# A hybrid encoder layer on one core: the scans' keys stored by step, and the broadcast rows of gates, maxima and factors fetched with one transfer per direction

## The chip, the cores and the metric

The kernel runs on one core of one Trainium2 chip. The core has a matrix engine (PE, whose weight loads are PEld), a vector engine (DVE), an activation engine (ACT), a general engine (POOL) and a queue engine (SP) that issues the transfers. Sixteen DMA engines carry the transfers. The metric is the device time of one execution in microseconds (us), lower is better.

## The reference, cut to what matters

One layer: a combined input projection feeds three head groups, whose outputs are concatenated, projected and added; then cross attention and a squared-ReLU MLP follow. What the change touches are the two scans, each run forward and backward over 16 double chunks of 128 tokens.

```python
h = rmsnorm(x, norm_mix_w[l])
... = jnp.split(h @ w_in[l], IN_OFFSETS, axis=-1)
y_na = neighbourhood_attention(...)      # local attention, 6 heads of 64
y_ml = mlstm_mixer(...)                  # 4 heads of 64, chunks of 64, two directions
y_gd = gated_deltanet_mixer(...)         # 6 heads of 64, chunks of 64, two directions
x = x + jnp.concatenate([y_na, y_ml, y_gd], axis=-1) @ w_out[l]
x = x + memory_cross_attention(...)
x = x + jnp.square(jax.nn.relu(h @ w_ff1[l])) @ w_ff2[l]

# inside gdn_direction, chunk by chunk
wk = jnp.einsum('bhnls,bhnsd->bhnld', t, kb * jnp.exp(gc)[..., None])
q_dec = q * jnp.exp(gc)[..., None]
# inside mlstm_direction, chunk by chunk
s_intra = jnp.einsum('bhnld,bhnsd->bhnls', q, k) * jnp.exp(dmat - m_t[..., None])
a_inter = jnp.exp(inter - m_t)
```

Here `gc` are the running sums of the gates, `m_t` the running maxima, `a_inter` the factors of the carried state.

## The kernel before

The program has two big parts. `mix` computes the three head groups; `tail` does the output projection, the cross attention and the MLP, and is nearly all matmul. `mix` again has two passes. `pass_a` projects the input, forms the chunks' matrices (`gram`, `inv`, `ml_prep`) and writes what the scans need to DRAM. `pass_b` runs the scans and the local attention, and reads it back.

`pass_b` is a loop over 16 steps that calls four generators by turns: `gdn_scan` (one step: chunk pair m forward and chunk pair 15 - m backward), `ml_scan` (the same for the other scan, one step later), `na` (three pieces of the local attention per step, 48 in all), and from step 9 on `heads_out`. The local attention so stands between scan steps and fills the engines. A scheduler with a model of the times turns the program into one order for each engine; each engine then runs its own list in order and waits on semaphores. All transfers of this part are issued by SP, in one list.

Each scan loads its step in a function `load(m)`, one step ahead. Both directions share a tile: one direction has partitions 0 to 63, the other 64 to 127 (`CH`, and `SR` for the other halves). Four of the tiles are filled by one transfer each for both directions:

- `kb` (scaled keys, 128 partitions x 768 floats, L645), from `kb_d`, which is laid out direction first, then step. The two rows wanted, forward m and backward 15 - m, are rows m and 31 - m of 32, so the source is a slice with a stride and has 2 as its outermost size, then 64 x 768.
- `ge` (running sums of gates, L646): one row of 768 floats per direction, repeated over 64 partitions; the source is 2 x 64 (repeated) x 768.
- `me` (running maxima, L850): the same with 512 floats.
- `mge` (factors of the state, L851): the same with 512 floats.

`kb`, `ge`, `qe`, `me`, `mge`, `mqe` and `mkq` have one buffer each, so the load of a step waits until the step before has read them. ACT takes the exponential of `ge` (L647), then POOL multiplies it into the queries (L650). DVE subtracts `me` from the column maxima (L852), POOL adds the mask (L853), ACT takes the exponential (L854), and DVE multiplies (L869). PE reads `kb` in L658. `both` (L664 to L666) is a helper that only issues the transfer, so the page puts `kb` and `ge` at L666.

In the last step, m = 15, the two rows of `kb_d` are rows 15 and 16, which lie side by side; there the `kb` transfer is one of 128 x 768 without the outer 2.

Of the kernel before, what the change touches and what calls it, by code (L numbers as in the profile page):

```python
# [38 lines left out]
class Trunk:  # L39
# [59 lines left out]
    def mix(self):  # L99

        tc, nc, I, dr = self.tc, self.nc, self.I, self.dr
        dt = lambda name, shape: dr.tile(shape, F32, name=name)
        self.y_d = [dt(f"y_d{b}", [8, P, 512]) for b in range(4)]
        self.gd_c = dt("gd_c", [9, P, T])
        self.gate_d = dt("gate_d", [5, P, T])
        self.mlc_d = dt("mlc_d", [16, P, 4, P])
        self.mlv_d = dt("mlv_d", [16, P, 4, 65])
        self.nac_d = dt("nac_d", [6, P, T])
        self.nav_d = dt("nav_d", [T, 384])
        self.g_row = dt("g_row", [16, 2, 2, 6, 64])  # L110
        self.sc_d = dt("sc_d", [2, 16, 2, 64, 2, 6, 64])
        self.kb_d = dt("kb_d", [2, 16, 64, 2, 6, 64])
        self.g_st = dt("g_st", [2, 16, 2, 6, 64])
        self.v_d = dt("v_d", [16, 2, 64, 6, 64])
        self.x_d = dt("x_d", [384, 64, 64])
        self.w_d = [[dt(f"w_d{d}{g}", [64, 12 * (b - a), 64]) for g, (a, b) in enumerate(GROUPS)] for d in range(2)]
        self.wt_d = [dt(f"wt_d{d}", [192, 32, 32]) for d in range(2)]
        with ExitStack() as big:
            self.c = big.enter_context(self.pool("mixc", 1))
            c = self.c  # L120
            self.ind2 = self.load_const("ind2", [P, 2])
            self.gmask = self.load_const("gmask", [P, 2, 64])
            self.egl = c.tile([P, 4, 2, 2, 4, 6], F32, name="egl")
            self.rr = c.tile([P, 16, 12], F32, name="rr")
            self.gcm = c.tile([P, 2, 16, 4], F32, name="gcm")
            self.gtm = c.tile([P, 2, 16, 4], F32, name="gtm")
            self.cm = c.tile([P, 2, 16, 4], F32, name="cm")
            self.cmx = c.tile([P, 2, 16, 4], F32, name="cmx")
            self.wxx = c.tile([P, 2, 16, 4], F32, name="wxx")
            self.emt = c.tile([P, 2, 16, 4], F32, name="emt")  # L130
            self.pass_a()
            self.pass_b()
# [282 lines left out]
    def gram(self, t):  # L415

        nc, pool = self.nc, self.tp
# [3 lines left out]
        e = pool.tile([P, 2, 6, 64], F32, name="gr")  # L421
# [49 lines left out]
        for d in range(2):  # L471
            sc = pool.tile([P, 3, 6, 64], F32, name="sc")
            V.tensor_tensor(out=byp(sc[:, 0]), in0=gv[:, :, :, 0:64], in1=byp(e[:, d]), op=ALU.mult)
            V.tensor_tensor(out=sc[:, 1], in0=heads(kt), in1=col(kst[:, d]), op=ALU.mult)
            V.tensor_tensor(out=sc[:, 2], in0=heads(kt), in1=col(self.eg[:, t, d]), op=ALU.mult)
            nc.sync.dma_start(out=self.sc_d[d, t].rearrange("c s a h l -> (c s) (a h l)"), in_=sc[:, 0:2].rearrange("p a h l -> p (a h l)"))
            for c2 in range(2):
                nc.sync.dma_start(out=self.kb_d[d, t, :, c2], in_=sc[64 * c2:64 * c2 + 64, 2])

    def inv(self, g, dirs, late=False):  # L480

# [140 lines left out]
    def gdn_scan(self, pool):  # L622
# [4 lines left out]
        nc, dr = self.nc, self.dr  # L627
        V, G = nc.vector, nc.gpsimd
        CH = (slice(0, 64), slice(64, 128))
        SR = (slice(64, 128), slice(0, 64))  # L630

        def load(m):
            wp = pool.tile([P, 2, 2, 6, 64], F32, name="wp")
            sc = pool.tile([P, 2, 2, 3, 6, 64], F32, name="sc")
            kb = pool.tile([P, 2, 6, 64], F32, name="kb", bufs=1)
            ge = pool.tile([P, 2, 6, 64], F32, name="ge", bufs=1)
            qe = pool.tile([P, 6, P], F32, name="qe", bufs=1)
            for d in range(2):
                t = m if d == 0 else 15 - m
                g = next(g for g, (a, b) in enumerate(GROUPS) if a <= t < b)  # L640
                nc.sync.dma_start(out=wp[CH[d], d].rearrange("p c h l -> p (c h) l"), in_=self.w_d[d][g][:, 12 * (t - GROUPS[g][0]):12 * (t - GROUPS[g][0]) + 12])
                nc.sync.dma_start(out=sc[CH[d], d, :, 0:2].rearrange("p c a h l -> p c (a h l)"), in_=self.sc_d[d, t].rearrange("c s a h l -> s c (a h l)"))
                nc.sync.dma_start(out=sc[CH[d], d, :, 2].rearrange("p c h l -> p c (h l)"), in_=self.v_d[t].rearrange("c s h l -> s c (h l)"))
                nc.sync.dma_start(out=qe[SR[d]], in_=self.gd_c[0:3, :, P * t:P * t + P].rearrange("c (h e) l -> e (c h) l", h=2))
            both(kb.rearrange("p c h l -> p (c h l)"), self.kb_d.rearrange("d t s c h l -> (d t) s (c h l)")[m:32 - m:31 - 2 * m])  # L645
            both(ge.rearrange("p c h l -> p (c h l)"), self.g_st.rearrange("d t c h l -> (d t) (c h l)")[15 - m:17 + m:2 * m + 1, None].broadcast_to([2, 64, 768]))  # L646
            nc.scalar.activation(out=ge, in_=ge, func=AF.Exp)  # L647
            for d in range(2):
                t = m if d == 0 else 15 - m
                G.tensor_tensor(out=sc[SR[d], d, :, 0], in0=qe[SR[d]].rearrange("p h (c l) -> p c h l", c=2), in1=ge[SR[d]], op=ALU.mult)  # L650
                V.tensor_tensor(out=sc[SR[d], d, :, 1], in0=self.ident[SR[d], None, None, SR[d]].broadcast_to([64, 2, 6, 64]),
                                in1=self.egl[SR[d], t // 4, :, d, t % 4, :, None].broadcast_to([64, 2, 6, 64]), op=ALU.mult)
            for i in range(2):
                ps = self.sps.tile([P, 512], F32, name="pss")
                for h in range(6):
                    for d in range(2):
                        c2 = i if d == 0 else 1 - i
                        nc.tensor.matmul(out=ps[SR[d], 64 * h:64 * h + 64], lhsT=kb[CH[d], c2, h], rhs=wp[CH[d], d, c2, h], start=True, stop=True)  # L658
                for d in range(2):
                    c2 = i if d == 0 else 1 - i  # L660
                    nc.scalar.copy(out=wp[SR[d], d, c2], in_=ps[SR[d], :384].rearrange("p (h x) -> p h x", x=64))
            return wp, sc

        def both(out, in_):  # L664

            nc.sync.dma_start(out=out, in_=in_)  # L666

        cur = load(0)
        yield
        for d in range(2):  # L670
            V.memset(cur[1][SR[d], d, d, 2], 0.0)
        evac = (V.tensor_copy, nc.scalar.copy)
        for m in range(16):
            nxt = load(m + 1) if m < 15 else None
            wp, sc = cur
            for i in range(2):
# [147 lines left out]
    def ml_scan(self, pool):  # L824
        tc, nc, dr = self.tc, self.nc, self.dr
        V, G = nc.vector, nc.gpsimd
        CH = (slice(0, 64), slice(64, 128))
        SR = (slice(64, 128), slice(0, 64))
# [7 lines left out]
        def load(m):  # L836

            sc = pool.tile([P, 2, 2, 2, 4, 64], F32, name="msc")
            r = pool.tile([P, 2, 2, 4, 65], F32, name="mr_")
            qe = pool.tile([P, 4, P], F32, name="mqe", bufs=1)  # L840
            ge = pool.tile([P, 4, P], F32, name="mge", bufs=1)
            kq = pool.tile([P, 2, 4, P], F32, name="mkq", bufs=1)
            e = pool.tile([P, 2, 4, 64], F32, name="me", bufs=1)
            for d in range(2):
                t = m if d == 0 else 15 - m
                nc.sync.dma_start(out=kq[:, d], in_=self.mlc_d[t])  # L846
                nc.sync.dma_start(out=r[CH[d], d].rearrange("p c h x -> p c (h x)"), in_=self.mlv_d[t].rearrange("(c s) h x -> s c (h x)", c=2))
                for a in range(2):
                    nc.sync.dma_start(out=qe[SR[d], a::2], in_=self.mlc_d[t, CH[a], 0:2])
            nc.sync.dma_start(out=e.rearrange("p c h l -> p (c h l)"), in_=self.mx_row.rearrange("d t c h l -> (d t) (c h l)")[m:32 - m:31 - 2 * m, None].broadcast_to([2, 64, 512]))  # L850
            nc.sync.dma_start(out=ge.rearrange("p h l -> p (h l)"), in_=self.ai_row.rearrange("d t h c l -> (d t) (h c l)")[15 - m:17 + m:2 * m + 1, None].broadcast_to([2, 64, 512]))  # L851
            V.tensor_tensor(out=e, in0=self.cmx[:, :, m, :, None].broadcast_to([P, 2, 4, 64]), in1=e, op=ALU.subtract)  # L852
            G.tensor_tensor(out=e, in0=e, in1=gm[:, None, None, :].broadcast_to([P, 2, 4, 64]), op=ALU.add)  # L853
            nc.scalar.activation(out=e, in_=e, func=AF.Exp)  # L854
# [16 lines left out]
            for d in range(2):  # L871
                t = m if d == 0 else 15 - m
# [3 lines left out]
            return sc, r  # L876

        cur = load(0)
        for d in range(2):
            V.memset(cur[1][SR[d], d, d], 0.0)  # L880
        evac = (V.tensor_copy, nc.scalar.copy)
        for m in range(16):
            nxt = load(m + 1) if m < 15 else None
            sc, r = cur
            for i in range(2):
# [531 lines left out]
```

## Time and profile before

| what | value |
|---|---|
| time before, median of 2 runs | 4129.35 us (4127.84 to 4130.86) |
| the profiled execution's own time | 4129.29 us |
| its span, first to last instruction | 4127.3 us |
| mean granted TensorE clock | 0.897 |
| busy: PE, PEld, DVE, ACT, POOL | 85%, 69%, 43%, 27%, 35% |
| transfers of queue 1 (SP's) | 375816 packets, 421.79 MB |

The page shows each engine's busy time over 40 slices, the transfers, the chain of work that ended last, and the costliest groups. In a group's row "x16" is the count; "a <- b" in a list of waits means that a stood idle until b was done. The chain names, step by step from the end back, what the work had waited for; a transfer in it counts from its issue to its landing. "SPq" is SP issuing a transfer.

### The profile page before, as it was taken

Reading aid. Unit: us, or ns where it says so; the run is one execution under the profiler, and the core shown is the slowest. Engines: PE = TensorE matmul, PEld = TensorE weight load, DVE = VectorE, ACT = ScalarE, POOL = GpSimd, SP = SyncE. Lnnn points to the kernel's source line nnn. Section 1 sums busy time; section 2 is a strip of 40 time slices with the busy share of each in tenths; the row PEclk is TensorE's granted clock in tenths of the full one; section 3 lists DMA queues with packets and bytes.
Section 4 is the critical chain, followed back from the end, with each engine's and each line's share of the span. In section 5 each row is a group of like instructions: output and inputs, shape, how many; then the busy total and the mean of one; then the engine's idle time right before and its main releaser. Section 6 shows DMA issues by size and latency. Waiting matters only on the chain.

```text
span 4127.3 us, 53735 instructions
## 1 busy us (share of the span) xinstructions
PE 3515.8 (85%) x21360; PEld 2830.8 (69%) x21360; DVE 1770.1 (43%) x3241; ACT 1122.2 (27%) x1976; POOL 1435.5 (35%) x876
## 2 busy tenths in 40 slices
PE   5988999895357566663999999999999999999998
PEld 4766777673235454442888888778888877888887
DVE  7767483741243345555443434532222244222224
ACT  3222422231122222221343333322221232221123
POOL 4242523441121112223544544433333354333333
PEclk8989999995576766775999999999999999999999
DMA  4476425855343454533333333321111132111112
GB/s 134 114 197 135 152 83 160 228 117 140 94 113 91 114 144 118 137 110 129 112 97 127 98 120 131 106 78 46 45 49 51 55 104 83 44 46 47 51 51 87
DMA packets 376610, 426.79 MB, mean 103 GB/s; under 512 B 150872, under 2 KB 277544, under 8 KB 374696
## 3 DMA queue, kind: packets, MB, share of 16 engines
q1 hardware_dynamic: 375816, 421.79, 34.8%
q8 instruction: 168, 2.75, 0.3%
q0 software_dynamic: 544, 1.57, 0.2%
q14 instruction: 82, 0.67, 0.1%
HBM read 331.16 MB, written 92.12 MB: 103 GB/s over the span
## 4 chain that ended last, share of the span: by engine, by line
PE 56%; DMA 13%; DVE 4%; SPq 3%; issue 2%; POOL 2%; ACT 1%; DVEq 0%; POOLq 0%; ACTq 0%
PE psg L95 31%; PE psa L95 19%; DMA ge<-g_st 4%; DMA me<-mx_row 3%; DMA wp<-w_d 1%; DMA y_d<-gz 1%; PE psn L977 1%; SPq L953 1%; PE psy L997 1%; PE psn L987 1%; DMA sc<-sc_d 1%; SPq L846 1%; DMA nav<-nav_d 0%; PE pss L688 0%; POOL wlo L1021 0%
## 5 line engine op out<-in xcount | busy, mean ns | idle before, releaser
L1021 POOL TENSOR_TENSOR wlo<-wraw,whi 128x1024 fp32r<-128x1024 f32 (+2 forms) x386 | 773.1, 2004 | 1367.0 <-ACT whi L1019 1328.7
L95 PE MATMUL psg<-acta,whi 128*128 128x512 f32 (+1 forms) x3008 | 951.9, 397 | 6.4 <-ACT acta L1160 3.2
L95 PE MATMUL psg<-actb,whi 128*128 128x512 f32 (+1 forms) x2752 | 841.6, 388 | 49.0 <-ACT actb L273 14.0
L1019 ACT CAST whi<-wraw 128x1024 fp32r<-128x1024 f32 (+2 forms) x402 | 358.1, 891 | 1230.6 <-PE psa L95 556.8
L95 PEld LDWEIGHTS psg<-acta,whi 128*128 128x128 f32 (+1 forms) x3008 | 567.8, 190 | 129.6 <-ACT acta L1160 4.0
L95 PE MATMUL psa<-ht,whi 128*128 128x512 f32 x2048 | 638.7, 395 | 0.7 <-ACT whi L1019 0.7
L95 PEld LDWEIGHTS psg<-actb,whi 128*128 128x128 f32 x2752 | 515.1, 192 | 158.1 <-ACT actb L273 14.7
L95 PE MATMUL psg<-acta,wlo 128*128 128x512 f32 (+1 forms) x1504 | 595.8, 397 | 1.8 <-POOL wlo L1021 1.8
L95 PE MATMUL psg<-actb,wlo 128*128 128x512 f32 (+1 forms) x1376 | 533.0, 387 | 4.7 <-POOL wlo L1021 4.2
L95 PEld LDWEIGHTS psa<-ht,whi 128*128 128x128 f32 x2048 | 384.1, 188 | 95.1 <-ACT whi L1019 1.6
L95 PE MATMUL psa<-ht,wlo 128*128 128x512 f32 x1024 | 400.8, 396 | 0.5 <-POOL wlo L1021 0.5
L1252 DVE TENSOR_TENSOR fr<-fr 128x512 f32<-128x512 f32 x128 | 167.8, 1311 | 495.6 <-ACT fr L1251 495.6
L1265 DVE TENSOR_TENSOR xb<-psa,xb 128x512 f32<-128x512 f32 x256 | 175.6, 691 | 475.9 <-PE psa L95 475.9
L95 PEld LDWEIGHTS psg<-acta,wlo 128*128 128x128 f32 (+1 forms) x1504 | 286.1, 190 | 64.4 <-POOL wlo L1021 3.3
L95 PEld LDWEIGHTS psg<-actb,wlo 128*128 128x128 f32 x1376 | 263.2, 191 | 57.4 <-POOL wlo L1021 5.8
L1255 POOL TENSOR_TENSOR ht<-fr,ht 128x512 fp32r<-128x512 f32 x128 | 168.9, 1320 | 250.2 <-ACT ht L1254 248.9
L95 PEld LDWEIGHTS psa<-ht,wlo 128*128 128x128 f32 x1024 | 192.2, 188 | 47.4 <-POOL wlo L1021 1.7
L853 POOL TENSOR_TENSOR me<-me,gm 128x512 f32<-128x512 f32 x16 | 21.1, 1320 | 456.9 <-DVE me L852 414.4
L987 PE MATMUL psn<-ident,nas 128*96 128x128 f32 (+1 forms) x336 | 75.6, 360 | 111.6 <-ACT nas L983 111.4
L308 DVE SCALAR_TENSOR_TENSOR acc<-pad,vecs,acc 128x512 f32<-128x512 f32 (+2 forms) x144 | 143.8, 1012 | 2.8
L1048 DVE TENSOR_TENSOR ss<-ss,sqt 128x512 f32<-128x512 f32 (+1 forms) x91 | 120.4, 1324 | 45.1 <-ACT sqt L1047 42.2
L997 PE MATMUL psy<-nap,nav 96*64 96x128 f32 (+2 forms) x672 | 89.3, 349 | 52.1 <-ACT nap L990 47.8
(376 smaller groups left out, 4042.3 us busy)
## 6 DMA issues: line engine op xcount, KB each, us to landing
wraw<-in_w_ff SPq DMA_DIRECT2D x72, 512.0 KB
wraw<-in_w_ff SPq DMA_DIRECT2D x144, 256.0 KB
wraw<-in_w_out SPq DMA_DIRECT2D x32, 512.0 KB
wraw<-in_w_xq SPq DMA_DIRECT2D x32, 512.0 KB
wraw<-in_w_xo SPq DMA_DIRECT2D x32, 512.0 KB
wraw<-in_w_gd SPq DMA_DIRECT2D x24, 512.0 KB
sc_d<-sc SPq DMA_DIRECT2D x32, 384.0 KB
sc<-sc_d SPq DMA_DIRECT2D x32, 384.0 KB
```

Source lines behind the costliest of these rows:

```text
L95: nc.tensor.matmul(out=out, lhsT=a(k), rhs=b(k), start=(i == 0), stop=(i == n - 1))
L308: V.scalar_tensor_tensor(out=acc[:, :n], in0=pad[:, p0 + j:p0 + j + n], scalar=cw(j), in1=acc[:, :n], op0=ALU.mult, op1=ALU.add)
L846: nc.sync.dma_start(out=kq[:, d], in_=self.mlc_d[t])
L953: nc.sync.dma_start(out=vw[:rows * ncl, j], in_=src)
L987: nc.tensor.transpose(out=tp[:n, P * j:P * j + P], in_=s[:, kt * j:kt * j + n], identity=self.ident)
L997: nc.tensor.matmul(out=yp[64 * e:64 * e + 64, P * hp:P * hp + P], lhsT=vw[:n, j, 128 * hp + 64 * e:128 * hp + 64 * e + 64], rhs=pts[e][:n, ...
L1019: nc.scalar.copy(out=hi, in_=raw)
L1021: (lo_eng or nc.gpsimd).tensor_tensor(out=lo, in0=raw, in1=hi.bitcast(F32), op=ALU.subtract)
L1048: nc.vector.tensor_tensor(out=ss, in0=ss, in1=sq, op=ALU.add)
L1252: V.tensor_tensor(out=r, in0=r, in1=r, op=ALU.mult)
L1255: G.tensor_tensor(out=ht[:, 1], in0=r, in1=ht[:, 0].bitcast(F32), op=ALU.subtract)
L1265: V.tensor_tensor(out=xs[nb][:, j], in0=ps, in1=xs[nb][:, j], op=ALU.add)
```

## The change

There are three edits, with the same numbers computed.

1. `kb_d` is laid out step first, then direction, where a backward chunk pair t is stored at step 15 - t. `gram` writes there with the same transfers of 64 x 384 floats. `load(m)` reads one contiguous block `kb_d[m]` as 128 rows of 768.
2. `ge` is filled by two transfers, one for each direction, each of 64 partitions x 768 with the source row repeated over 64 as the outermost size.
3. `me` and `mge` the same, each by two transfers of 64 x 512, in one loop over the directions.

```diff
-        self.kb_d = dt("kb_d", [2, 16, 64, 2, 6, 64])
+        self.kb_d = dt("kb_d", [16, 2, 64, 2, 6, 64])
...
-                nc.sync.dma_start(out=self.kb_d[d, t, :, c2], in_=sc[64 * c2:64 * c2 + 64, 2])
+                nc.sync.dma_start(out=self.kb_d[15 - t if d else t, d, :, c2], in_=sc[64 * c2:64 * c2 + 64, 2])
...
-            both(kb.rearrange("p c h l -> p (c h l)"), self.kb_d.rearrange("d t s c h l -> (d t) s (c h l)")[m:32 - m:31 - 2 * m])
-            both(ge.rearrange("p c h l -> p (c h l)"), self.g_st.rearrange("d t c h l -> (d t) (c h l)")[15 - m:17 + m:2 * m + 1, None].broadcast_to([2, 64, 768]))
+            both(kb.rearrange("p c h l -> p (c h l)"), self.kb_d[m].rearrange("d s c h l -> (d s) (c h l)"))
+            for d in range(2):
+                nc.sync.dma_start(out=ge[SR[d]], in_=self.g_st[1 - d, 15 - m if d else m][None].broadcast_to([64, 2, 6, 64]))
...
-            nc.sync.dma_start(out=e.rearrange("p c h l -> p (c h l)"), in_=self.mx_row.rearrange("d t c h l -> (d t) (c h l)")[m:32 - m:31 - 2 * m, None].broadcast_to([2, 64, 512]))
-            nc.sync.dma_start(out=ge.rearrange("p h l -> p (h l)"), in_=self.ai_row.rearrange("d t h c l -> (d t) (h c l)")[15 - m:17 + m:2 * m + 1, None].broadcast_to([2, 64, 512]))
+            for d in range(2):
+                t = m if d == 0 else 15 - m
+                nc.sync.dma_start(out=e[CH[d]], in_=self.mx_row[d, t][None].broadcast_to([64, 2, 4, 64]))
+                nc.sync.dma_start(out=ge[SR[d]].rearrange("p h l -> p (h l)"), in_=self.ai_row[1 - d, t].rearrange("h c l -> (h c l)")[None].broadcast_to([64, 512]))
```

In `ml_scan` the tile called `ge` in the code is `mge` in the rows, and `e` is `me`.

The scheduler runs again on the changed program. On SP, in the middle of the scans, the list reads before (`wp`, `sc`, `qe`, `kb`, `ge` belong to the one scan, `mr`, `mqe`, `mge`, `mkq`, `me` to the other, `naqb` to the attention):

```order
L644 DMA qe<-gd_c 64x6x128 x2
L666 DMA kb<-kb_d 128x1x768
L666 DMA ge<-g_st 128x1x768
L849 DMA mqe<-mlc_d 64x2x128 x4
L851 DMA mge<-ai_row 128x1x512
L956 DMA naqb<-nac_d 128x3x128
L641 DMA wp<-w_d_85 64x768
L641 DMA wp<-w_d_90 64x768
L846 DMA mkq<-mlc_d 128x512 x2
L850 DMA me<-mx_row 128x1x512
```

and at the same place in the changed program:

```order
L644 DMA qe<-gd_c 64x6x128 x2
L667 DMA kb<-kb_d 128x768
L647 DMA ge<-g_st 64x768 x2
L850 DMA mqe<-mlc_d 64x2x128 x4
L854 DMA mge<-ai_row 64x512 x2
L959 DMA naqb<-nac_d 128x3x128
L641 DMA wp<-w_d_85 64x768
L641 DMA wp<-w_d_90 64x768
L847 DMA mkq<-mlc_d 128x512 x2
L853 DMA me<-mx_row 64x512 x2
```

The sequence is the same; `ge`, `mge` and `me` are two issues each, and `kb` has lost its outer size.

On ACT, in one of the early steps, the list reads before (`nas` and `nap` are the attention, `wp`, `sc`, `acc` the one scan's copies out of PSUM, `ge` and `me` the two exponentials):

```order
L700 COPY acc<-pss 64x384
L647 ACTIVATE ge<-ge 128x768
L990 COPY nap<-psn 128x384
L992 COPY nap<-psn 96x128
L683 COPY sc<-pss 64x384
L983 ACTIVATE nas,nsm<-nas,nam 128x480 x2
L700 COPY acc<-pss 64x384
L691 COPY sc<-pss 64x384
L990 COPY nap<-psn 128x384
L992 COPY nap<-psn 96x128
L661 COPY wp<-pss 64x384 x4
```

and at the same place in the changed program:

```order
L701 COPY acc<-pss 64x384
L648 ACTIVATE ge<-ge 128x768
L897 COPY mr__9067<-psl 64x260
L993 COPY nap<-psn 128x384
L995 COPY nap<-psn 96x128
L684 COPY sc<-pss 64x384
L986 ACTIVATE nas,nsm<-nas,nam 128x480
L692 COPY sc<-pss 64x384
L701 COPY acc<-pss 64x384
L857 ACTIVATE me<-me 128x512
L993 COPY nap<-psn 128x384
```

The exponential of `me` and a copy of `mr` have moved up, ahead of attention copies (`nap`, `nas`) that stood before them.

## Rows read from the trace of the kernel before

**Rows 1.** The page: span, and tenths in 40 slices: PE busy, clock granted.
```profile
span 4127.3 us, 53735 instructions
...
PE   5988999895357566663999999999999999999998
...
PEclk8989999995576766775999999999999999999999
```

**Rows 2.** By stretch: us; busy us (xcount) PE, PEld, DVE, ACT, POOL; clock, DMA, GB/s.
```profile
1112.00:1667.00 555.00, 351.97 (x4152) 259.76 (x4154) 239.13 (x564) 141.60 (x365) 111.55 (x73) 0.69 0.43 116
...
960.00:1945.00 985.00, 548.38 (x6352) 405.17 (x6348) 419.51 (x1043) 220.88 (x553) 197.72 (x130) 0.66 0.42 115
```

**Rows 3.** The chain, 960 to 1945 us: by line; first and last piece of `ge`.
```profile
by line: DMA ge<-g_st 16.2%; DMA me<-mx_row 13.3%; DMA wp<-w_d 4.2%; issue 4.0%; DMA y_d<-gz 3.9%; PE psn L977 3.4%; PE psy L997 2.9%; PE psn L987 2.6%; SPq L953 2.3%; DMA sc<-sc_d 2.1%; SPq L846 2.1%; DMA nav<-nav_d 2.0%; PE pss L688 2.0%;
...
1111.74 18.84 DMA ge<-g_st
...
1561.57 18.74 DMA ge<-g_st
```

**Rows 4.** Waits of ACT, then DVE, then PE, 960 to 1945 us: total, times, longest.
```profile
ACT ge L647 <- DMA ge<-g_st: 272.4, 16, 28.3
...
DVE me L852 <- DMA me<-mx_row: 195.9, 16, 38.8
...
PE psn L987 <- ACT nas L983: 111.4, 21, 19.3
```

**Rows 5.** By stretch: `ge` in flight, then `mge`, then four transfers of `gr`.
```profile
1311.00:1316.00 5.00, 0.00 (x0) 0.00 (x0) 0.00 (x0) 0.00 (x0) 0.00 (x0) 0.50 0.13 52
1318.00:1322.00 4.00, 3.09 (x15) 2.62 (x16) 1.31 (x3) 2.24 (x7) 0.00 (x0) 0.50 0.13 51
...
212.00:215.00 3.00, 3.00 (x14) 2.46 (x14) 2.83 (x6) 0.00 (x0) 1.56 (x1) 1.00 0.77 212
```

**Rows 6.** The transfers' sizes, from the list of issues.
```profile
kb<-kb_d SPq DMA_DIRECT2D x16, 384.0 KB
ge<-g_st SPq DMA_DIRECT2D x16, 384.0 KB
me<-mx_row SPq DMA_DIRECT2D x16, 256.0 KB
...
gr<-g_row SPq DMA_DIRECT2D x32, 192.0 KB
```

**Rows 7.** SP in order of time, one step: start, us, what.
```profile
1296.93 0.55 SPq L666 DMA_DIRECT2D kb<-kb_d  x1
1297.56 2.37 SPq L666 DMA_DIRECT2D ge<-g_st  x1
1300.03 9.09 SPq L849 DMA_DIRECT2D mqe<-mlc_d  x4
1309.17 0.52 SPq L851 DMA_DIRECT2D mge<-ai_row  x1
...
1325.51 0.52 SPq L850 DMA_DIRECT2D me<-mx_row  x1
```

**Rows 8.** ACT, DVE, PE in order of time in that step; brackets: idle before.
```profile
1317.33 0.84 ACT L647 ACTIVATE ge<-ge 128x768 f32<-128x768 f32 x1 [18.66 <-DMA ge<-g_st]
...
1320.30 0.56 DVE L700 COPY acc<-pss 64x384 f32<-64x384 f32 x1 [16.20 <-ACT acc L700]
...
1318.91 1.11 PE L987 MATMUL psn<-ident,nas 128*128 128x128 f32 x4 [14.34 <-ACT nas L983]
```

**Rows 9.** The chain: the first and the last piece of `me`.
```profile
1077.54 16.46 DMA me<-mx_row
...
1852.20 8.37 DMA me<-mx_row
```

**Rows 10.** Issues by line: count, ns min/median/max, first and last start.
```profile
L666 SPq DMA_DIRECT2D ge<-g_st x16: 517/2093/5105, 995.5 to 1698.3; - x16
...
L849 SPq DMA_DIRECT2D mqe<-mlc_d x64: 573/608/6250, 961.0 to 1830.7; - x64
```

## The prediction

> **What bounds the kernel now.** I read the page first, for where time is lost. Its slices show PE at 9 tenths in the last half, the tail, and at 3 to 7 tenths in slices 11 to 19 [rows 1]. Those slices are pass B, the scans with the local attention between them. The busy times by stretch put numbers to it: from 960 to 1945 us, 985 us, PE is busy for 548.4 us, DVE for 419.5, ACT for 220.9, POOL for 197.7; the mean clock is 0.66, a mix of the two levels, 1.2 and 2.4 GHz; and all DMA engines together are busy for 0.42 of the time [rows 2]. No engine is full, and the transfers aren't either. Something is late.
>
> The chain of waits over the same stretch says what: 16.2% of it is the landing of `ge`, 13.3% that of `me`, then `wp`, and so on, with PE's own lines at 2 to 3.4% each [rows 3]. So 0.162 x 985 = 160 us and 0.133 x 985 = 131 us of the chain are these two broadcasts. The lists of waits agree: ACT stood 272.4 us for `ge` in 16 waits, DVE 195.9 us for `me` in 16 [rows 4]. Both engines run in order, so all behind the wait stands too. One step shows it: ACT stands 18.66 us for `ge`, DVE, whose next copy follows one of ACT, 16.20 us for ACT, and PE 14.34 us for an exponential of the attention that is queued behind `ge` on ACT [rows 8]. Over the whole stretch PE waits 111.4 us for these exponentials, L983 [rows 4].
>
> Why is a transfer of 384 KB [rows 6] so slow? The step in [rows 7] issues `kb` and `ge` at 1297 us and `mge` at 1309, and nothing from then until 1324. While `ge` is still in flight, the DMA share is 0.13 and the rate 52 GB/s; once it has landed, at 1317.3, and `mge` streams, 0.13 and 51 GB/s [rows 5]. 0.13 of 16 engines is two engines. The outermost size of these sources is 2, one row for each direction. `gr` in pass A is also one row repeated over 64 partitions, in two transfers of 64 partitions (192 KB each [rows 6]): four of them move at 212 GB/s with a share of 0.77 [rows 5]. That is the form `ge`, `me` and `mge` get. The new `kb` has 128 rows outermost, and I price it like `gr`.
>
> **The change part by part.**
>
> *Streaming time.* 384 KB is 393,216 bytes: 7.6 us at 52 GB/s, 1.9 us at 212. 256 KB is 262,144 bytes: 5.1 us at 51 GB/s, 1.2 us at 212. A step has `kb` and `ge` (384 KB) and `me` and `mge` (256 KB, the same shape): 2 x 7.6 + 2 x 5.1 = 25.4 us before and 6.2 after. On the same two engines, 25.4 us is half of a step: the 16 issues of `ge` lie 702.8 us apart from first to last, 46.9 us a step [rows 10].
>
> *`ge` on the chain.* The last piece of `me`, 8.37 us from issue to landing [rows 9], has little beside it; 5.1 of it is streaming, so 3.3 us are fixed. The chain has eight pieces of `ge`, from 18.84 us the first to 18.74 the last [rows 3], 160 / 8 = 20 us each: its own 7.6, the 7.6 of `kb` right ahead of it [rows 7], 3.3 fixed, and some queueing. After: 3.3 fixed, 0.6 for the second issue (the shortest issues last 0.52 and 0.57 us [rows 10]), and 1 to 2 us of streaming: 5.5 us. The chain loses 8 x 14.5 = 116 us.
>
> *`me` on the chain.* 131 us in 11 pieces, from 16.46 us the first, behind other transfers, to 8.37 the last [rows 9], 12 us each. After: 3.3 + 0.6 + 0.6 = 4.5 us. The chain loses 131 - 11 x 4.5 = 82 us.
>
> *What stood behind them.* Every other transfer has a share on the two crowded engines, so it lands after them. The chain has 4.2% on `wp`, 2.1% on `sc`, 2.0% on `nav` [rows 3]: 82 us. SP also stands while it issues: right after `kb` and `ge`, four issues of `mqe` take 9.09 us, with 0.608 the median of one [rows 7, 10], and all that SP's list has behind them waits. SP L953 and L846 are 4.4% of the chain, 43 us [rows 3]. None of this is the change's own row, so I bound it: nothing at one end, two thirds of 82 + 43 = 125 us, 83 us, at the other (the rest is these transfers' own fixed time). I take 60, as the step in rows 7 shows the mechanism plainly.
>
> *What is added.* 48 more issues on SP, in three lines, 0.6 us each: 29 us on SP, which in 985 us has room. SP's list keeps its sequence around them, as the first pair of order rows shows. On the path they count one issue per wait, and that is in the sums above. The writes of `kb_d` have the same size and number: nothing, and `gram` lies in pass A, beside matmuls that keep PE at 8 to 9 tenths [rows 1]. If a write were late there it would have to delay the first load of the scan, hundreds of us after.
>
> *The reordering.* On ACT the exponential of `me` moves ahead of attention copies, as the second pair of order rows shows. With `me` landing in 4.5 us that is harmless; were it as late as before, the copies behind it would wait for it too. I take nothing, with bounds of 3 us either way in each of 16 steps, 48 us.
>
> *The sum.* 116 + 82 + 60 = 258 us off the chain. That isn't all gain, since another chain is then the longest. After the full 258, pass B would last 727 us with 548 us of PE work, 75% busy. The best long stretch of it now, 1112 to 1667 us, has 352 of 555, 63%, at clock 0.69 [rows 2], with waits of the very kind that go. PE's work also shrinks when the clock stays at its upper level, which it does in the tail, 9 in all slices [rows 1], where PE has no holes; at 0.66 there is room for it, but holes of some us remain. I therefore cut the sum by a fifteenth, to 240 us: pass B lasts 745 us, PE 73% busy at today's durations. 4127.3 - 240 = 3887.3 us of span, plus 2.0 around it (4129.29 less 4127.3): 3889 us. The median of the runs shown, 4129.35, is the profiled execution's time to 0.1 us.
>
> **The rivals.**
>
> *A new wait takes half of it.* With the broadcasts on time, the attention's own chain (scores on PE, minimum on DVE, exponential on ACT, transposes on PE, copies on ACT or DVE) and the scans' evacuations become the step. For it: PE already waits 111.4 us for L983 [rows 4]. Against it: much of that is ACT standing at `ge`, as in rows 8. If PE got no denser than the 63% of rows 2, pass B would last 548 / 0.63 = 870 us: 115 us gained, 4014 us. I give gains of 83 to 180 us 0.22.
>
> *The chain gives more.* If the transfers behind give their upper bound (83) and the reordering its good end (48), 116 + 82 + 83 + 48 = 329 us: 3800 us. It needs PE at 548 / 656 = 84%, or a faster clock. Gains over 310 us: 0.12.
>
> *The halves serialize.* Two transfers of 64 partitions each would stream one after the other at the old rate: 3.8 + 3.8 us for `ge`. Only `kb` would then be faster, by 5.7 us in each of eight `ge` pieces, 46 us, less up to 29 us of issues: 17 to 46 us gained, 4083 to 4112 us. Against it stand the four `gr` at 212 GB/s [rows 5]. The Trainium skill, DMA: Bandwidth & Descriptors, "Rules for kernel authors", says of two transfers to disjoint partition halves "Don't bother — they serialize", because both halves spread over all 16 engines in any case. By that rule the splits would bring nothing and the time would be some 4100 us; the trace's 0.13 shows that the one transfer here isn't spread so, and by the rows it is 3889. With every other small gain, 0.04.
>
> *Slower.* The reordered ACT list puts a late `me` in front of attention and scan copies. If each `me` were 20 us late in ACT's place (the longest wait now is 38.8 us [rows 4]), 16 x 20 = 320 us would be lost against 240 gained: 80 us slower, 4209 us. It decides from 15 us a step. At 4.5 us a landing it can't come near: 0.02.
>
> **How the numbers follow.** The forecast, a gain of 180 to 310 us, has 0.60. The likeliest point is 3889 us. Its own range is 3819 to 3949. For 8 in 10 I add most of the two neighbours: 3800 to 4000. A difference of 2%, 83 us, is about what a measurement of this kernel can tell from no change. Faster by more than that is 0.60 + 0.22 + 0.12 = 0.94; within it 0.04; slower 0.02.
>
> **What would show each step right or wrong.** In the profile after, the chain's pieces of `ge` and `me` should be 4 to 7 us each, their waits on ACT and DVE below 80 us each in total, and a stretch with a broadcast in flight should no longer sit at a share of 0.13. The median issue of `ge` should fall from 2.1 us to 0.6, and no `mqe` group should take 9 us. PE's clock in pass B should rise above 0.66. If the waits shrink so but pass B stays above 850 us, the step on the next bound is wrong; if the broadcasts still take over 10 us, the step on the two engines is.

## The result, and the profile after

The changed kernel takes 3882.68 us (median of 2 runs, 3877.90 to 3887.45) against 4129.35, a ratio of 0.940 with an interval of 0.935 to 0.945: 247 us gained, where 240 were forecast. In the same numbers as before, its profiled execution took 3887.45 us with a span of 3885.5.

The page of the changed kernel, in the form of [rows 1]:

```profile
span 3885.5 us, 53790 instructions
...
PE   4988999898678888449999999999999999999998
...
PEclk8998999998677777669999999999999999999999
```

Most slices of pass B, at 3 to 7 tenths before, are now at 6 to 8, and there are fewer of them; two at 4 remain, 1554 to 1748 us, at its end. Where pass B ends is read from the tail's first cast of what the passes have written, `acta<-yr` (count, shortest, median and longest in ns, first and last start). Before:

```profile
L1160 ACT CAST acta<-yr x32: 611/618/627, 1946.4 to 2451.1; 128x512 fp32r<-128x512 f32 x32
```

and after:

```profile
L1163 ACT CAST acta<-yr x32: 608/622/630, 1709.5 to 2215.2; 128x512 fp32r<-128x512 f32 x32
```

The first load of the scans is `mkq`, before and after:

```profile
959.25 0.47 SPq L846 DMA_DIRECT2D mkq<-mlc_d  x1
...
965.35 0.47 SPq L847 DMA_DIRECT2D mkq<-mlc_d  x1
```

From there to the tail's first cast, pass B went from 987 us to 744. What follows it takes 4127.3 - 1946.4 = 2181 us and 3885.5 - 1709.5 = 2176. The whole gain lies in pass B.

The stretches of the changed kernel, columns as in [rows 2]. The first two answer to [rows 2], the last two to the stretches of `ge` and `mge` in [rows 5]: `kb` and `ge`, then `me`, are in flight there beside other loads.

```profile
1112.00:1667.00 555.00, 418.66 (x5087) 305.62 (x5083) 345.61 (x853) 175.77 (x443) 151.96 (x99) 0.73 0.57 146
960.00:1705.00 745.00, 528.85 (x6376) 389.48 (x6376) 427.32 (x1043) 222.12 (x555) 201.41 (x130) 0.70 0.59 152
...
1240.00:1245.00 5.00, 5.00 (x36) 3.15 (x38) 1.26 (x3) 0.10 (x2) 0.00 (x0) 0.50 0.75 193
1250.00:1254.00 4.00, 4.00 (x59) 2.60 (x58) 3.25 (x9) 1.52 (x4) 0.00 (x0) 1.00 0.78 210
```

Over 745 us PE is busy for 528.9, 71%, with the clock at 0.70 instead of 0.66. The share of the DMA engines with a broadcast in flight is 0.75 and 0.78, 193 and 210 GB/s, in place of 0.13 and 51 to 52. Other loads have a part in the new figures.

The issues by line (count, ns min/median/max, first and last start), as in [rows 10], and SP in order of time in one step, as in [rows 7]:

```profile
L647 SPq DMA_DIRECT2D ge<-g_st x32: 467/477/1627, 995.4 to 1481.2; - x32
...
L850 SPq DMA_DIRECT2D mqe<-mlc_d x64: 573/605/1693, 967.1 to 1596.3; - x64
```

```profile
1238.41 0.56 SPq L667 DMA_DIRECT2D kb<-kb_d  x1
1239.80 2.11 SPq L647 DMA_DIRECT2D ge<-g_st  x2
1242.54 2.55 SPq L850 DMA_DIRECT2D mqe<-mlc_d  x4
...
1245.77 1.12 SPq L854 DMA_DIRECT2D mge<-ai_row  x2
...
1250.10 1.09 SPq L853 DMA_DIRECT2D me<-mx_row  x2
```

The four `mqe` behind `ge` are issued in 2.55 us, where [rows 7] has 9.09.

The waits of ACT, DVE and PE (total, times, longest), as in [rows 4]:

```profile
ACT ge L648 <- DMA ge<-g_st: 88.3, 15, 11.5
...
DVE me L855 <- DMA me<-mx_row: 63.6, 14, 15.4
...
PE psn L990 <- ACT nas L986: 45.4, 23, 5.0
```

And the chain over pass B, as in [rows 3] and [rows 9], with the first and last pieces of `me` and `ge`:

```profile
by line: PE psn L980 6.7%; PE psy L1000 5.6%; DMA sc<-sc_d 5.2%; DMA me<-mx_row 5.0%; issue 4.9%; DMA ge<-g_st 4.8%; PE psn L990 4.7%; DMA nav<-nav_d 3.0%; PE psl L866 3.0%; PE pss L689 3.0%; PE psl L870 2.7%; DVE sc L652 2.6%; DMA y_d<-gz 
...
977.85 4.30 DMA me<-mx_row
995.40 8.69 DMA ge<-g_st
...
1384.16 5.50 DMA ge<-g_st
...
1619.06 4.38 DMA me<-mx_row
```

`ge` has 0.048 x 745 = 36 us in six pieces, 6.0 us each, and `me` 0.050 x 745 = 37 us in eight, 4.7 us each. PE's own lines now lead.

### The profile page after: what moved, and what is told of

The parts are those of the page before. It is cut to its first block, busy times and chain, and to the rows that moved or that the text cites. A ratio compares the mean times of both kernels' runs of the same rounds, so it can differ in the third digit from the quotient of the medians.

```text
span 3885.5 us, 53790 instructions
## 1 busy us (share of the span) xinstructions
PE 3489.0 (90%) x21360; PEld 2807.7 (72%) x21360; DVE 1781.9 (46%) x3241; ACT 1123.7 (29%) x1976; POOL 1441.0 (37%) x876
## 4 chain that ended last, share of the span: by engine, by line
PE 59%; DMA 7%; DVE 7%; POOL 2%; issue 2%; SPq 2%; ACT 1%; DVEq 0%; POOLq 0%; ACTq 0%
PE psg L95 32%; PE psa L95 20%; PE psn L980 1%; PE psy L1000 1%; DMA sc<-sc_d 1%; DMA me<-mx_row 1%; DMA ge<-g_st 1%; PE psn L990 1%; DVE x L501 1%; DVE tv L500 1%; DMA nav<-nav_d 1%; PE psl L866 1%; PE pss L689 1%; PE psl L870 1%; POOL x L501 0%
## 5 line engine op out<-in xcount | busy, mean ns | idle before, releaser
L1051 DVE TENSOR_TENSOR ss<-ss,sqt 128x512 f32<-128x512 f32 (+1 forms) x91 | 121.5, 1336 | 43.5 <-ACT sqt L1050 40.5
L1257 ACT CAST ht<-fr 128x512 fp32r<-128x512 f32 x128 | 79.7, 623 | 180.3 <-DVE fr L1255 180.2
L856 POOL TENSOR_TENSOR me<-me,gm 128x512 f32<-128x512 f32 x16 | 21.1, 1316 | 252.1 <-DVE me L855 100.4
L1254 ACT ACTIVATE fr<-psg 128x512 f32<-128x512 f32 x128 | 76.0, 594 | 132.1 <-PE psg L95 132.1
```

The costliest lines, as they stand in the source:

```text
L1051: nc.vector.tensor_tensor(out=ss, in0=ss, in1=sq, op=ALU.add)
L1254: S.activation(out=r, in_=ps, func=AF.Relu)
L1257: S.copy(out=ht[:, 0], in_=r)
```

## The experiments

The forecast's theory is that the four transfers with 2 as their outermost size run on two DMA engines, and that this makes them late, and what stands behind them. Its rivals are that the other order of the work brings the gain, or the number of transfers, and that only the wait for each transfer's own landing counts. The engines' orders matter for reading the single parts: in `e1_kb` they are those of before in all but a few rows, while `e2_ge` and `e3_me` each get a new order from the scheduler, so their gains hold whatever that does too.

**One part alone.** In `e1_kb` only the keys are laid out by step:

```diff
-            both(..., self.kb_d.rearrange("d t s c h l -> (d t) s (c h l)")[m:32 - m:31 - 2 * m])
+            both(..., self.kb_d[m].rearrange("d s c h l -> (d s) (c h l)"))
```

> The keys alone: kb_d by step, kb read as 128 rows; ge, me and mge stay one transfer each with 2 outermost. The engines' orders are those of before (DVE's and POOL's the same, PE's in all but a few rows). Two-engine theory: kb streams in 1.9 us instead of 7.6, and ge, right behind it on the same two engines, lands 5.7 us sooner in each of its eight chain pieces: 46 us, and a quarter of the 60 us of what stood behind: 61 us gained, 4068 us, 4040 to 4100. Rival, the gain comes from the scheduler's new order: nothing, 4129 us, 4115 to 4143. Rival, each transfer's own landing alone counts: kb is waited for seldom (26 us on PE), so 4100 to 4129 us.

Measured: 4041.52 us (4034.68 to 4046.59), ratio 0.978 (0.977 to 0.980), against 4130.07 of the kernel before on that chip: 88.6 us. That is within the range of the two-engine theory, and faster than either rival allows, 4100 us at best. In `e2_ge` only `ge` is split:

```diff
-            both(ge..., self.g_st...[15 - m:17 + m:2 * m + 1, None].broadcast_to([2, 64, 768]))
+            for d in range(2):
+                nc.sync.dma_start(out=ge[SR[d]], in_=self.g_st[1 - d, 15 - m if d else m][None].broadcast_to([64, 2, 6, 64]))
```

> The gates alone: ge in two transfers, one for each direction; kb, me and mge as before. Two-engine theory: ge streams on 16 engines, but a sixteenth of each half still queues behind kb on the crowded two, so its pieces fall from 20 us to about 13: 8 x 7 = 56 us, and a quarter of 60: 71 us gained, 4058 us, 4030 to 4095. Rival, order: the engines' orders differ from both others, so it makes no statement. Rival, own landing alone counts: the whole 116 us of ge, 4013 us.

Measured: 4074.74 us (4071.91 to 4079.40), ratio 0.987 (0.985 to 0.988): 55.3 us, within the range of the two-engine theory; 4013 us, for own landing alone, is ruled out. In `e3_me` only `me` and `mge` are split:

```diff
-            nc.sync.dma_start(out=e..., in_=self.mx_row...broadcast_to([2, 64, 512]))
-            nc.sync.dma_start(out=ge..., in_=self.ai_row...broadcast_to([2, 64, 512]))
+            for d in range(2):
+                t = m if d == 0 else 15 - m
+                nc.sync.dma_start(out=e[CH[d]], in_=self.mx_row[d, t][None].broadcast_to([64, 2, 4, 64]))
+                nc.sync.dma_start(out=ge[SR[d]]..., in_=self.ai_row[1 - d, t]...[None].broadcast_to([64, 512]))
```

> The maxima and factors alone: me and mge in two transfers each; kb and ge as before. Two-engine theory: 82 us of me on the chain, less where it queues behind kb and ge, and two fifths of 60: 80 to 106 us gained, 4023 to 4050 us. Rival, order: most of the changed program's order is this edit's, so most of the gain, about 3900 us. Rival, own landing alone: 82 us, 4047 us.

Measured: 4060.46 us (4054.95 to 4064.71), ratio 0.983 (0.982 to 0.985): 69.6 us. This is 10 us slower than the expected 4023 to 4050, and 13 slower than the 4047 of own landing alone, so it doesn't tell these two apart; the rival of the order, about 3900, is far off. The waits of ACT for `ge` and of DVE for `me` say how the three work. In `e1_kb`:

```profile
ACT ge L647 <- DMA ge<-g_st: 182.8, 16, 21.9
...
DVE me L852 <- DMA me<-mx_row: 170.4, 16, 32.2
```

in `e2_ge`:

```profile
ACT ge L648 <- DMA ge<-g_st: 193.6, 16, 23.2
...
DVE me L853 <- DMA me<-mx_row: 172.5, 16, 28.6
```

and in `e3_me`:

```profile
ACT ge L647 <- DMA ge<-g_st: 282.5, 16, 24.9
...
DVE me L854 <- DMA me<-mx_row: 104.1, 10, 30.8
```

Before, they are 272.4 and 195.9 us [rows 4]. A faster `kb` takes 89.6 us from the wait for `ge`, though `ge` itself is untouched. The wait falls in 15 of the 16 steps, by 6.0 us on average, about the 7.6 - 1.9 = 5.7 us of streaming of the `kb` ahead. In the last step, where `kb` had no outer 2 before either, it is the same, before and in `e1_kb`:

```profile
1714.05 0.84 ACT L647 ACTIVATE ge<-ge 128x768 f32<-128x768 f32 x1 [11.00 <-DMA ge<-g_st]
...
1625.58 0.84 ACT L647 ACTIVATE ge<-ge 128x768 f32<-128x768 f32 x1 [11.00 <-DMA ge<-g_st]
```

A faster `ge` alone takes about as much from that wait (78.8 us) and 23 us from `me`'s. A faster `me` leaves the wait for `ge` where it was. So a transfer of this kind delays what is issued behind it. The single gains sum to 88.6 + 55.3 + 69.6 = 214 us, and the whole change has 247; what the other 33 are wasn't separated.

**Order and number, with two engines kept.** `e4_cols` is the changed kernel with the keys by step, but `ge`, `me` and `mge` are cut into two column halves, each for both directions, so 2 stays the outermost size. It issues as many transfers as the changed kernel and its lists are close to the changed kernel's (63 rows differ on PE, 17 on ACT and 16 on DVE; before and after differ in about 590 on PE).

```diff
-            for d in range(2):
-                nc.sync.dma_start(out=ge[SR[d]], in_=self.g_st[1 - d, 15 - m if d else m][None].broadcast_to([64, 2, 6, 64]))
+            for x in (slice(0, 384), slice(384, 768)):
+                both(ge...[:, x], self.g_st...[15 - m:17 + m:2 * m + 1, None, x].broadcast_to([2, 64, 384]))
```

> As the changed kernel, but ge, me and mge are cut by columns instead of by direction: two transfers each, as many issues, half the columns each, and both keep 2 as the outermost size of the source. The engines' orders are nearly the changed program's (PE's list differs in 63 rows, against some 590 between before and after). Two-engine theory: these three stay on two engines, the DMA share with one in flight stays 0.13, and the time is that of the keys alone, 4068 us, up to 60 us more for twice the packets: 4050 to 4130. Rival, order or the number of transfers: as the changed kernel, 3883 us, 3865 to 3905.

Measured: 4065.06 us (4054.66 to 4071.51), ratio 0.984 (0.982 to 0.986). By stretch (first a half of `ge` alone in flight, then a half of `mge`; columns as in [rows 2]) and by waits:

```profile
1386.00:1388.00 2.00, 0.00 (x0) 0.00 (x0) 0.00 (x0) 0.00 (x0) 0.00 (x0) 0.50 0.13 51
1390.00:1392.00 2.00, 0.62 (x3) 0.60 (x4) 0.00 (x0) 1.98 (x6) 0.00 (x0) 0.50 0.14 49
```

```profile
ACT ge L648 <- DMA ge<-g_st: 194.6, 15, 22.9
...
DVE me L854 <- DMA me<-mx_row: 189.6, 16, 37.7
```

The share is 0.13 again, the time is in the range of the two-engine theory, and the waits are near those of `e1_kb` (12 and 19 us longer). With 2 still outermost, the new order and the second issues bring no gain, and about 182 us of the gain hang on which size stands outermost in three transfers.

**The same transfers, with nobody waiting for them.** `e5_crowd` adds to the changed kernel 64 transfers of the old form, from DRAM to DRAM, which nothing reads.

```diff
+            for n in range(2):
+                nc.sync.dma_start(out=self.crowd_d[m, n], in_=self.g_st...[15 - m:17 + m:2 * m + 1, None].broadcast_to([2, 64, 768]))
...
+            for n, row in enumerate((self.mx_row..., self.ai_row...)):
+                nc.sync.dma_start(out=self.crowd_d[m, 2 + n, :, :, :512], in_=row[15 - m:17 + m:2 * m + 1, None].broadcast_to([2, 64, 512]))
```

> The changed kernel, and beside each of its loads of kb, ge, me and mge one more transfer of the old form, two rows repeated over 64 (two of 384 KB and two of 256 KB a step), from DRAM to a DRAM tensor that nobody reads, so nobody waits for it. It does 64 transfers more than the kernel and changes none of its values. The scheduler's orders differ from both kernels. Theory that the two crowded engines delay all that has a share on them: most of the gain that own landing doesn't explain goes, and ge and me themselves land late behind the new traffic: 3950 to 4080 us, with long issues on SP again. Rival, only the landing of the transfer itself counts: 64 issues of 0.6 us at most, 3883 to 3925 us.

Measured: 4220.99 us (4213.94 to 4227.02), ratio 1.021 (1.020 to 1.023); on the same chip the changed kernel ran again as `after2`, 3875.84 us (3860.89 to 3877.70), ratio 0.937 (0.935 to 0.939). The cost is far above both expectations, and it lies elsewhere: with no reader to wait for, the scheduler put the added issues ahead of pass B, into pass A and the gap behind it. Their issues in `e5_crowd` (count, ns min/median/max, first and last start):

```profile
L650 SPq DMA_DIRECT2D crowd_d<-g_st x32: 581/3678/11964, 653.1 to 918.8; - x32
...
L859 SPq DMA_DIRECT2D crowd_d<-mx_row x16: 585/4174/7162, 1032.7 to 1194.1; - x16
```

The stretch from 640 to 962 us in `e5_crowd`:

```profile
640.00:962.00 322.00, 141.11 (x630) 112.67 (x632) 45.69 (x123) 25.47 (x37) 47.41 (x23) 0.68 0.31 99
```

and in the changed kernel:

```profile
640.00:962.00 322.00, 291.07 (x2169) 235.23 (x2165) 161.73 (x410) 80.06 (x122) 130.62 (x105) 0.93 0.65 169
```

Where an issue of `ge` takes 0.48 us at its median, these take 3.7 or 4.2. By their place SP seems unable to go on until the two engines have taken in what lies ahead, which this run alone doesn't show; everything SP issues behind it comes late, and PE does 141 us of work in place of 291. The first load of pass B is issued about 320 us later, at 1280.9 us, and pass B itself takes 756 us. That the transfers hold up work which shares nothing with them but SP and the engines is shown; by how much in pass B isn't, since they weren't there.

**The crowd within pass B.** For that, `e8_two` puts one such transfer behind each finished block of the local attention, 16 in pass B, and `e9_spread` the same bytes at the same places, with 384 outermost. The lists of PE, DVE and ACT are the same in the two; on SP only the added rows differ.

```diff
 e8_two
+            nc.sync.dma_start(out=self.crowd_d[4 * rb + cb], in_=self.y_d[rb][0:2, 0:1, P * cb:P * cb + P].broadcast_to([2, 384, 128]))
 e9_spread
+            nc.sync.dma_start(out=self.crowd_d[4 * rb + cb].rearrange("j r l -> r j l"), in_=self.y_d[rb][0:2, 0:1, P * cb:P * cb + P].broadcast_to([2, 384, 128]).rearrange("j r l -> r j l"))
```

> The changed kernel plus one transfer of 384 KB behind each finished block of the local attention (16 in pass B), from DRAM to DRAM, which nobody reads: a row of 128 floats of each of two heads' pairs repeated 384 times, with 2 as the outermost size. Its twin below moves the same bytes at the same places of SP's list with 384 outermost; the lists of all other engines are the same in the two. If a transfer with 2 outermost holds up the others (the landings and SP's issues behind it), 16 x (4 to 6 us) = 64 to 96 us are lost, by what the keys alone gave (88.6 us for 16 such transfers): 3935 to 3975 us against 3875.8 of the changed kernel. If only the wait for the transfer itself counts, nobody waits here: 16 x 0.6 us of issue, 3876 to 3895, as the twin. Stretch with it alone in flight: DMA share 0.13.

> The same transfers, bytes and places as in the run before, with 384 as the outermost size. Both theories: 16 issues of 0.6 us and 2 us of streaming each, 3876 to 3895 us. If the bytes or the wait of SP for the finished block cost, and not the two engines, it is as slow as its twin.

Measured: `e8_two` 3986.15 us (3981.77 to 3988.10), ratio 0.965 (0.964 to 0.967); `e9_spread` 3927.21 us (3917.16 to 3940.17), ratio 0.950 (0.949 to 0.952). One of the added transfers, with SP's next issue, and a stretch with it in flight, in `e8_two`:

```profile
1251.34 0.61 SPq L1014 DMA_DIRECT2D crowd_d<-y_d  x1
1252.01 8.87 SPq L957 DMA_DIRECT2D nav<-nav_d  x1
```

```profile
1255.00:1261.00 6.00, 6.00 (x38) 3.64 (x37) 2.18 (x6) 0.79 (x2) 0.00 (x0) 0.50 0.14 44
```

and the same in `e9_spread`:

```profile
1244.44 0.61 SPq L1014 DMA_DIRECT2D crowd_d<-y_d  x1
1245.10 0.74 SPq L957 DMA_DIRECT2D nav<-nav_d  x1
```

```profile
1248.00:1250.00 2.00, 2.00 (x24) 1.15 (x18) 0.85 (x3) 0.23 (x2) 0.00 (x0) 1.00 0.30 75
```

With 2 outermost the share is 0.14, and SP stands 8.87 us in the next issue, of `nav`; 384 KB at 44 GB/s are 8.9 us. With 384 outermost that issue takes 0.74 us. So it goes behind all 16: the next issue takes 4.41 to 10.57 us in `e8_two`, 134 us together, and 0.61 to 0.74 us in `e9_spread`, 11 together. `e8_two` is 59 us slower than its twin, 3.7 us for each transfer, though nobody waits for it, and 11 us beyond the slow end of what was expected. The chain of `e8_two` has 5.9% of 830 us, 49 us, in SP's issue of `nav`:

```profile
by line: DMA y_d<-gz 6.6%; DMA ge<-g_st 6.4%; SPq L957 5.9%; issue 5.9%; DMA y_d<-nat 4.8%; PE psn L981 4.7%; PE psn L991 3.7%; PE psy L1001 3.6%; DMA me<-mx_row 3.1%; DMA gz<-gate_d 3.0%; DMA qe<-gd_c 2.8%; DMA wp<-w_d 2.7%; PE pss L690 2.
```

Over pass B, SP's issues make up 104 us of the chain in `e8_two` and 27 in `e9_spread`, the landings of transfers 294 and 308. So here the cost shows as SP standing, and not as other transfers landing later.

The twin's own expectation missed: it is some 50 us above the changed kernel, not 20 at most. Its added transfer isn't as quick as `ge`: 0.30 and 75 GB/s. Which of its short rows, the one row that all of them read, or DRAM as its target makes it so wasn't tried, so the 59 us are two engines against this twin, not against a transfer that is spread as well as `ge`.

**What is left.** `e6_nav_rows` loads `nav` with one transfer for each row of the grid:

```diff
-                nc.sync.dma_start(out=vw[:rows * ncl, j], in_=src)
+                for x in range(rows):
+                    nc.sync.dma_start(out=vw[ncl * x:ncl * x + ncl, j], in_=src[x])
```

> The changed kernel, and the attention's values (nav), whose source has 4 or 3 grid rows outermost, are loaded by one transfer for each grid row, with 32 or 24 tokens outermost. Two-engine theory carried on: nav ran on four engines and has 22.7 us of the chain in two pieces; spread over more engines it gains up to 20 us, but SP has some 150 more issues of 0.6 us, 90 us in a list that has waits behind it: 3870 to 3920 us, 3890 likeliest. Rival, that the issues cost nothing: 3865 us.

Measured: 3866.46 us (3856.45 to 3868.76), ratio 0.935 (0.934 to 0.937), 9 us below `after2` with intervals that overlap: no difference that this shows, and 4 us below the expected range, near the rival's 3865. `e7_geme_act` lets ACT's queue issue `ge` and `me` in the changed kernel:

```diff
-                nc.sync.dma_start(out=ge[SR[d]], ...
+                nc.scalar.dma_start(out=ge[SR[d]], ...
...
-                nc.sync.dma_start(out=e[CH[d]], ...
+                nc.scalar.dma_start(out=e[CH[d]], ...
```

> The changed kernel, and ge and me are issued by ACT instead of SP. If what is left of their waits (ACT 88 us for ge, DVE 64 us for me) is that SP's list issues them late, behind other loads that wait for their buffers, they come sooner and 20 to 60 us are gained: 3823 to 3863 us. If what is left is the one buffer that each has, so that the load can't start before the step before has read it, or ACT stands before the issue, nothing or up to 40 us slower: 3880 to 3920 us.

Measured: 3847.03 us (3845.50 to 3850.66), ratio 0.931 (0.930 to 0.933): 29 us below `after2`, in the range expected if SP's list issues the two late. ACT's wait for `ge` is 89.0 us in `after2`. It halves in `e7_geme_act`, but also in `e6_nav_rows`, where SP still issues `ge`:

```profile
ACT ge L648 <- DMA ge<-g_st: 43.7, 10, 8.7
...
ACT ge L648 <- DMA ge<-g_st: 44.1, 10, 11.4
```

DVE's wait for `me`, 69.6 us in `after2`, is 40.5 in `e7_geme_act` and still 68.7 in `e6_nav_rows`. So the 29 us can't be put down to the wait for `ge` alone; how much of them is SP having come late to either issue wasn't separated. `e10_both` has the edits of these two:

> The changed kernel with ge and me issued by ACT's queue (3847.0 us alone, 29 less) and nav loaded by one transfer for each row of the grid (3866.5 alone, 9 less). If the two gains are of different waits they add: 3838 us (3825 to 3855). If both only shorten the same wait on SP, or the added nav issues on SP are what is late next, 3845 to 3870.

Measured: 3807.14 us (3800.40 to 3828.76), ratio 0.923 (0.920 to 0.926), the fastest of all, and below both expected ranges. In the stretch of pass B, and in the two waits:

```profile
960.00:1625.00 665.00, 480.91 (x6366) 358.37 (x6363) 419.03 (x1042) 220.10 (x554) 198.25 (x129) 0.78 0.68 172
```

```profile
ACT ge L648 <- DMA ge<-g_st: 27.4, 10, 6.1
...
DVE me L855 <- DMA me<-mx_row: 46.6, 13, 8.9
```

The two edits alone took 0.0059 and 0.0020 from the ratio of 0.9372 that `after2` has, which would make 0.929; 0.923 lies below that by more than its interval. PE needs 480.9 us for the same work at clock 0.78, where the changed kernel needs 528.9 at 0.70, and its idle time in pass B falls from 216 us to 184. Why `nav` by rows, which shows little alone, helps so much here wasn't separated.

## Why the prediction was right

*The two engines.* Right. A share of 0.13 could also be all 16 engines busy for an eighth of the time, but the single packets in the trace before, 1311 to 1316 us, come in two unbroken rows: there are never fewer than two under way, and three for only 0.3 of the 5 us. The share became 0.75 and 0.78, and with 2 put back as the outermost size in three of the four transfers, `e4_cols`, it is 0.13 again and three quarters of the gain are gone.

*`ge` and `me` on the chain.* The pieces were to be 5.5 and 4.5 us and are 6.0 and 4.7; the chain loses 160 - 36 = 124 us and 131 - 37 = 94, where 116 and 82 stood. There are also fewer pieces, 6 for 8 and 8 for 11. ACT's wait for `ge`, 88.3 us, is a little over the 80 that the prediction allowed.

*What stood behind them.* Taken as 60 us, with bounds of 0 and 83. The transfers that were named hardly moved: `wp`, `sc<-sc_d` and `nav` together have 82 us on the chain before and 76 after (`wp` fell from 42 to 14, `sc` rose from 21 to 39). The two lines of SP's issues that were named, of `nav` and `mkq`, fell from 43 to 7 us. That is 6 + 36 = 42 us, less than the 60. But SP's issues as a whole fell from 107 to 33 us over the pieces of the chain in pass B, 38 more than the named two, and other transfers that weren't in the sum (`sc<-v_d`, `mge` and the store `y_d` among them) gave 34 more. Together that is 114 us, beyond the upper bound. The larger part is SP standing in its issues, which the prediction had from one row, the 9.09 us in [rows 7], and priced with the rest.

*The cut.* This step was mis-sized, and it hid the term above. All transfers lose 257 us on the chain and SP 74, 331 in all; PE's pieces grow by 50 and DVE's by 38. So 88 us, a quarter, are given back to the next chain, where the prediction took a fifteenth of 258, 18 us. 331 - 88 = 243 us, and 258 - 18 = 240. The mechanism was right, but that the sum is right to 3 us is luck: the prediction had 73 us too little coming off the chain, and 70 too little coming back. PE's busy share came out at 71%, not 73%, with PE's work at 529 us instead of 548, at the higher clock.

*The keys.* `e1_kb` gives 88.6 us where 61 were expected, 46 on the pieces of `ge` and 15 behind them. On its chain the eight pieces of `ge` fall from 159 to 113 us, which is the 46. SP's issues fall from 107 to 64, 43 us instead of 15. So what was too small is again SP standing behind such transfers.

*What is added, and the reordering.* Nothing was taken for them, and nothing larger than 24 us shows: `e4_cols`, with the second issues and nearly the new order, is 24 us slower than `e1_kb`, which has its keys and neither. Those 24 us are on the side of a loss, within the bounds of 48, and what of them the issues, the order or the smaller pieces are wasn't separated. `me` is still late there (189.6 us of waits), so what the new order is worth with `me` on time no run shows.

*The rivals.* A new wait at half of the gain didn't come: PE's wait for the attention's exponentials fell from 111.4 to 45.4 us with ACT's wait, as [rows 8] had it. The halves don't stream one after the other at the old rate: with those of `me` in flight it is 210 GB/s. The Trainium skill, DMA: Bandwidth & Descriptors, "Rules for kernel authors", says that two transfers to disjoint partition halves aren't worth it. Here they are, as `e2_ge` with 55 us and `e3_me` with 70 show. The single transfer they replace wasn't spread, and cutting it by columns, which leaves it so, gains nothing over the keys alone (`e4_cols`). The same page of the Trainium skill says under "Use all 16 engines" that an outermost dimension of size c below 16 confines a transfer to at most c engines. The trace agrees, 0.13 with 2 outermost against 0.75 and 0.78 with 64 and 128.

## What to carry to other kernels

Where transfers are late though the DMA engines are mostly idle, read the share in a stretch with one alone in flight: 0.13 is two engines, and the outermost size of the source or target is the first thing to look at. Such a transfer is paid by everything that is issued behind it, and by SP, which stands in its next issue; price SP's standing as a term of its own, over all its issues, and not from the lines that the chain names first. Gains taken off a chain are partly given back to the next one, here a quarter.

## What was not expected of the hardware

SP's issue is not always short: behind a transfer of 384 KB that runs on two engines the next issue stood 8.87 us in `e8_two`, the time that the transfer takes at 44 GB/s, and in `e5_crowd`, where several stood in a row, an issue took 3.7 to 4.2 us at its median and up to 12.0. In the kernel before and after it shows as well: the four `mqe` behind `kb` and `ge` took 9.09 us and then 2.55. What holds SP there, the profile doesn't name. And a transfer that repeats two rows 384 times from DRAM to DRAM stayed at a share of 0.30, 75 GB/s, though its outermost size is 384; why is open.
